# Products of probabilities and values in the opposite order within a batch

## The chip, the cores and the metric

The kernel runs on one core of one Trainium2 chip. The metric is the device time of one execution in microseconds. The kernel before takes 1553.61 us, the median of three runs (1551.71 to 1553.72).

## What is computed

Two layers of a streaming encoder. Each normalises its input, projects it, sends the projection through three parallel groups (a short convolution, latent attention with 8 heads, an RWKV-7 recurrence), gates each group, projects the concatenated output and adds the input. There are 1104 rows: 64 of a running stream with 256 cached rows, 16 meta rows and 1024 rows of a new stream. The change touches the last step of the attention:

```
s = jnp.where(vis[None, None], s, NEG)
p = jax.nn.softmax(s, axis=-1).astype(v.dtype)
return jnp.einsum('bhqk,bkhd->bqhd', p, v)
```

Attention is causal over chunks of 64 rows, so a query block sees all key blocks up to its own. Head width of the values is 64. Everything is float32.

## The kernel before

The heads are taken in four pairs. For a pair, the queries come in five units: u = -1 (the 64 rows of the running stream and the 16 meta rows) and u = 0 to 3 (256 rows each). Four generators of `attention` work on these: `scores` makes the scores of one head and unit, their maximum, exponential and scaling, and leaves probability tiles `p` with queries on the partitions; `transpose` turns them with TensorE into a PSUM bank `tr`, one bank for each job, and evicts the bank to a tile `pt` with keys on the partitions; `outputs` multiplies `pt` with the values `v` into the PSUM tile `po`; `prepare` makes keys, queries and values.

`jobs(u)` lists what is multiplied: for u >= 0 the meta keys, then 2u + 1 blocks of 128 keys that both halves of the 256 queries see (256 columns of `po`), then one block that only the later 128 queries see (columns 128 to 256). For u = -1 there are three entries in two jobs, all over 80 columns. So a pair has 20 entries of 256 columns, 4 of 128 and 3 of 80; with four pairs and two layers that is 160, 32 and 24. Each entry needs two products, one for each head of the pair: head j = 0 goes to partitions 0 to 63 of `po`, j = 1 to 64 to 127. That makes 432 products; a float32 product stands as two records in the trace.

`outputs` takes the jobs of a unit in batches of at most BATCH = 5, here called goes: 3 jobs in one go for u = 0, 5 for u = 1, 4 and 3 for u = 2, 5 and 4 for u = 3, 2 for u = -1. A pair has 7 goes, the program 56. JOBS = 7 tiles `pt` exist. Once the unit is done, VectorE multiplies `po` with the gate into `yo`, which is written to memory; the output projection reads it back later (`yraw`).

Two things set the order. First the generators are stepped by the program's own estimate of when things are due (`race`, `due`, class Meter), so that a go is recorded as one piece; `fill` is the part of the output projection that needs no attention (`prj<-yhi,wo` and `prj<-ylo,wo`), taken where nothing else is due. Then the framework under it schedules the recorded instructions on each engine's queue: of those that it takes to be ready it issues the one that was recorded first, so that a recorded piece can be taken apart. All instructions go through one helper, so line 81 stands for nearly all of them, and tiles' names tell them apart.

Of the kernel before, what the change touches and what calls it, by code (L numbers as in the profile page):

```python
# [194 lines left out]
class Net:  # L195
# [518 lines left out]
    def attention(self, l):  # L714
# [113 lines left out]
        def jobs(u):  # L828

            if u < 0:  # L830
                n = PAD0
                return [[(0, 128, 0, n, 0, True, False), (1, 128, 2 * n, n, 0, False, False)], [(2, n, 0, n, 0, False, True)]]
            x = [[(3, 128, 0, 256, 0, True, False)]]
            x += [[(4 + k, 128, 0, 256, 0, False, False)] for k in range(2 * u + 1)]
            return x + [[(4 + 2 * u + 1, 128, 0, 128, 128, False, True)]]
# [23 lines left out]

        def outputs():  # L860
            for pr, u in units:
                todo, po = jobs(u), None
                while todo:
                    size = -(-len(todo) // -(-len(todo) // BATCH))
                    batch, todo = todo[:size], todo[size:]
                    blocks = [b for js in batch for b, *_ in js]
                    yield (lambda: len(turned) >= count["jobs"] + size and all((pr, 4 * (b // 4) if b > 3 else 0 if b < 2 else b) in valued for b in blocks),)
                    ts = turned[count["jobs"]:count["jobs"] + size]
                    yield *ts, *(self.v[b][:k] for js in batch for b, k, *_ in js), *(() if po else ("po",))
                    po = po or self.ps("po", "po")  # L870
                    for t, js in zip(ts, batch):
                        for b, k, c, m, o, start, stop in js:
                            for j in range(2):
                                r = slice(64 * j, 64 * j + 64)
                                self.mm(po[r, o:o + m], self.v[b][:k, r], t[:, c + j * m:c + (j + 1) * m], start=start, stop=stop)
                    count["jobs"] += size
                q0, n = span(u)
                yo = self.small("yo", [128, 256], bufs=2)
                nc.vector.tensor_tensor(out=yo[:, :n], in0=po[:, :n], in1=gates[pr, u][:, :n], op=ALU.mult)
                nc.sync.dma_start(self.yd[4 + pr, :, q0:q0 + n], yo[:, :n])  # L880
                count["out"] += 1
# [653 lines left out]
```

## Time and profile before

| | |
|---|---|
| median of three runs | 1553.61 us |
| the profiled execution | 1553.56 us |
| its span, first to last instruction | 1551.8 us |
| matmuls on TensorE | 1476.9 us, 95% of the span |
| VectorE, ScalarE, GpSimd | 69%, 50%, 17% |
| mean granted TensorE clock | 0.989 |

Attention's products stand in two stretches of the span, one in each layer: about 466 to 710 us and 1228 to 1470 us. A record of a matmul has a start that was measured and an end that is modelled, so times below are taken from a record's start to the start of the next one.

### The profile page before, as it was taken

To read this page: it belongs to the slowest core of one execution; us is meant where nothing else is said; L and a number is where in the kernel's file an instruction comes from. 1 tells how busy PE (TensorE), PEld (TensorE's weight loads), DVE (VectorE), ACT (ScalarE), POOL (GpSimd) and SP (SyncE) were. 2 spreads that over 40 slices of the span, in tenths; PEclk is the share of its full clock that TensorE was granted. 3 is DMA by queue.
4 is the path that set the end of the run, shared out by engine and by line. 5 is a ranking of instruction groups with operands and counts; after the bars stand their busy time and mean duration, and the time that the engine had idled before them with its cause. 6 is when DMAs were issued, how large, how long until landed. Compare 5 with 4: busy or idle time off the path is not lost.

```text
span 1551.8 us, 30755 instructions
## 1 busy us (share of the span) xinstructions
PE 1476.9 (95%) x12060; PEld 1311.2 (84%) x12060; DVE 1065.6 (69%) x2623; ACT 769.8 (50%) x1842; POOL 256.5 (17%) x281
## 2 busy tenths in 40 slices
PE   7999998998999999999999998899999999999996
PEld 7988887987887878879999887798988878778795
DVE  7576596675868766675845575776867787676566
ACT  7135454444577565563522354444356775565442
POOL 0221221311221101100011222312212301011002
PEclk9999999999999999999999999999999999999998
DMA  6332112222324101211323311212222331102123
GB/s 218 123 113 68 52 54 60 83 52 57 92 94 152 38 26 33 68 57 62 147 93 103 110 45 49 70 48 81 69 65 65 115 120 46 31 19 84 47 65 117
DMA packets 95328, 119.82 MB, mean 77 GB/s; under 512 B 41872, under 2 KB 74768, under 8 KB 95184
## 3 DMA queue, kind: packets, MB, share of 16 engines
q1 hardware_dynamic: 95184, 117.87, 24.6%
q8 instruction: 95, 1.56, 0.4%
q14 instruction: 49, 0.40, 0.1%
HBM read 81.24 MB, written 36.60 MB: 76 GB/s over the span
## 4 chain that ended last, share of the span: by engine, by line
PE 65%; DVE 17%; ACT 7%; issue 5%; DMA 3%; POOL 2%; SPq 0%; DVEq 0%; POOLq 0%; ACTq 0%
PE prj L81 31%; PE sc L81 7%; PE po L81 7%; PE tr L81 5%; PE upq L81 3%; DVE tri L81 3%; PE inv L81 2%; DVE wq L81 2%; PE val L81 1%; DVE wlo L81 1%; ACT wq L81 1%; PE upk L81 1%; DVE st L81 1%; DVE cv L81 1%; PE w L81 1%
## 5 line engine op out<-in xcount | busy, mean ns | idle before, releaser
L81 PE MATMUL prj<-hhi,whi 128*128 128x384 f32 (+1 forms) x1152 | 391.7, 340 | 7.5 <-ACT hhi L81 6.6
L81 PE MATMUL prj<-hlo,whi 128*128 128x384 f32 (+1 forms) x1152 | 390.7, 339 | 0.6 <-DVE hlo L81 0.6
L81 PE MATMUL prj<-hhi,wlo 128*128 128x384 f32 (+1 forms) x1152 | 390.4, 339 | 0.2 <-DVE wlo L81 0.2
L81 PEld LDWEIGHTS prj<-hhi,whi 128*128 128x128 f32 x1152 | 218.9, 190 | 11.0 <-ACT hhi L81 6.6
L81 PEld LDWEIGHTS prj<-hlo,whi 128*128 128x128 f32 x1152 | 218.7, 190 | 4.9 <-DVE hlo L81 1.0
L81 PEld LDWEIGHTS prj<-hhi,wlo 128*128 128x128 f32 x1152 | 218.7, 190 | 3.3 <-issue 0.5
L81 PE MATMUL prj<-yhi,wo 128*128 128x384 f32 (+2 forms) x776 | 207.0, 337 | 0.9 <-DVE xn L81 0.9
L81 PE MATMUL sc<-ka,qa 128*128 128x264 f32 (+8 forms) x720 | 152.4, 334 | 2.3 <-ACT p L81 2.0
L81 ACT ACTIVATE p<-sc,st 128x144 f32<-128x144 f32 (+8 forms) x240 | 128.1, 542 | 50.4 <-DVE st L81 49.3
L81 PEld LDWEIGHTS prj<-yhi,wo 128*128 128x128 f32 x776 | 138.4, 188 | 4.8 <-DVE xn L81 2.4
L81 DVE TENSOR_REDUCE st<-sc 128x1 f32<-128x144 f32 (+8 forms) x240 | 118.0, 502 | 24.3 <-PE sc L81 22.4
L81 PE MATMUL prj<-ylo,wo 128*128 128x384 f32 (+2 forms) x388 | 130.6, 337 | 0.0
L81 ACT ACTIVATE pt<-tr 128x512 f32<-128x512 f32 (+3 forms) x172 | 90.0, 544 | 77.6 <-PE tr L81 76.3
L81 PEld LDWEIGHTS sc<-ka,qa 128*128 128x128 f32 (+1 forms) x720 | 112.2, 187 | 19.0 <-ACT p L81 6.1
L81 PE MATMUL tr<-cst,p 128*128 128x128 f32 (+2 forms) x752 | 115.7, 277 | 3.3 <-ACT pt L81 1.7
L81 PE MATMUL po<-pt,v 128*64 128x256 f32 (+3 forms) x864 | 110.7, 357 | 0.0
L81 PEld LDWEIGHTS tr<-cst,p 128*128 128x128 f32 (+2 forms) x752 | 83.5, 140 | 25.6 <-issue 7.6
L81 POOL TENSOR_TENSOR qa<-qt,qa 128x512 fp32r<-128x512 f32 (+1 forms) x40 | 47.3, 1184 | 349.3 <-ACT qa L81 349.3
L81 ACT ACTIVATE whi<-wraw 128x1024 fp32r<-128x1024 f32 x48 | 50.7, 1056 | 82.6 <-PE prj L81 64.9
L81 DVE TENSOR_TENSOR tri<-tri 48x14 f32<-48x14 f32 (+6 forms) x336 | 82.2, 245 | 9.1 <-DMA tri<-tri 0.3
L81 PEld LDWEIGHTS po<-pt,v 128*64 128x64 f32 (+1 forms) x864 | 56.6, 136 | 33.5 <-issue 11.6
L81 DVE TENSOR_SCALAR p<-p,st 80x336 f32<-80x336 f32 (+5 forms) x144 | 81.5, 568 | 1.9
(227 smaller groups left out, 2639.9 us busy)
## 6 DMA issues: line engine op xcount, KB each, us to landing
wraw<-w_in SPq DMA_DIRECT2D x48, 512.0 KB, 3.6
wraw<-w_out SPq DMA_DIRECT2D x32, 256.0 KB, 2.6
zd<-z SPq DMA_DIRECT2D x14, 576.0 KB, 3.4
wr<-zd SPq DMA_DIRECT2D x36, 192.0 KB, 3.0
gd<-gate SPq DMA_DIRECT2D x12, 552.0 KB, 3.1
yraw<-yd SPq DMA_DIRECT2D x8, 552.0 KB, 4.0
xn<-x SPq DMA_DIRECT2D x8, 552.0 KB, 3.9
xd<-xn SPq DMA_DIRECT2D x8, 552.0 KB, 3.0
```

The lines of the kernel that those rows point to most:

```text
L81: r = f(*args, **kw)
```

## The change

Within a go the entries are taken in the opposite order: the newest tile first, the oldest last. The start flag, which clears the accumulator, is now set on the first product of a unit for each of the two heads (`seen`), and the stop flag on the last product of the unit; the check of accumulation groups at build time is off for these products, since the first product of some units covers only columns 128 to 256.

```
-                todo, po = jobs(u), None
+                todo, po, seen = jobs(u), None, set()
...
-                    for t, js in zip(ts, batch):
-                        for b, k, c, m, o, start, stop in js:
-                            for j in range(2):
-                                r = slice(64 * j, 64 * j + 64)
-                                self.mm(po[r, o:o + m], self.v[b][:k, r], t[:, c + j * m:c + (j + 1) * m], start=start, stop=stop)
+
+                    xs = [(t, *x) for t, js in zip(ts, batch) for x in js][::-1]
+                    for i, (t, b, k, c, m, o, _, _) in enumerate(xs):
+                        for j in range(2):
+                            r = slice(64 * j, 64 * j + 64)
+                            self.mm(po[r, o:o + m], self.v[b][:k, r], t[:, c + j * m:c + (j + 1) * m], start=j not in seen,
+                                    stop=not todo and i == len(xs) - 1, group=False)
+                            seen.add(j)
```

The order of TensorE's instructions around it changes as well. The first place is the second go of unit u = 2 of the first pair in the first layer: `po_5658` is its accumulator, `pt_5630`, `pt_5656` and `pt_5670` its tiles in the order of their making, `tr_5667` the bank that is evicted to `pt_5670`. Before:

```order
L81 MATMUL tr_5667<-cst,p_5418 128x128
L81 MATMUL tr_5667<-cst,p_5493 128x128
L81 MATMUL prj_5647<-yhi_5621,wo_5246 128x336
L81 MATMUL po_5658<-pt_5630,v_5033 64x256
L81 MATMUL sc_5679<-ka_4791,qa_5296 128x16
L81 MATMUL sc_5679<-ka_4792,qa_5296 128x16
L81 MATMUL sc_5679<-ka_4791,qa_5296 128x16
L81 MATMUL po_5658<-pt_5630,v_5033 64x256
L81 MATMUL po_5658<-pt_5656,v_5033 64x256 x2
L81 MATMUL po_5658<-pt_5670,v_5033 64x128 x2
```

At the same place the changed kernel has:

```order
L81 MATMUL tr_5667<-cst,p_5418 128x128
L81 MATMUL tr_5667<-cst,p_5493 128x128
L81 MATMUL sc_5679<-ka_4791,qa_5296 128x16
L81 MATMUL sc_5679<-ka_4792,qa_5296 128x16
L81 MATMUL sc_5679<-ka_4791,qa_5296 128x16
L81 MATMUL upq_5722<-cqhi_4996,uq_5444 128x336
L81 MATMUL upq_5722<-cqlo_4998,uq_5444 128x336
L81 MATMUL upq_5722<-cqhi_4996,uq_5444 128x336
L81 MATMUL po_5658<-pt_5670,v_5033 64x128 x2
L81 MATMUL po_5658<-pt_5656,v_5033 64x256 x2
L81 MATMUL po_5658<-pt_5630,v_5033 64x256 x2
```

The go stood in two pieces, with one product of `pt_5630` on each side of a score, and stands in one now; query products (`upq`) moved in front of it.

The second place is on TensorE too, near the end of the first layer's attention: the second go of unit u = 3 of the last pair, with `po_8008`, and `pt_8029` as its newest tile, evicted from `tr_8026`. Before:

```order
L81 MATMUL tr_8026<-cst,p_7874 128x128
L81 MATMUL tr_8026<-cst,p_7924 128x128
L81 MATMUL prj_7963<-yhi_5621,wo_7275 128x384
L81 MATMUL po_8008<-pt_7998,v_5033 64x256 x2
L81 MATMUL po_8008<-pt_8006,v_5033 64x256 x2
L81 MATMUL po_8008<-pt_8024,v_5033 64x256 x2
L81 MATMUL po_8008<-pt_8029,v_5033 64x128 x2
```

The changed kernel has there:

```order
L81 MATMUL tr_8026<-cst,p_7874 128x128
L81 MATMUL tr_8026<-cst,p_7924 128x128
L81 MATMUL prj_7963<-yhi_5621,wo_7275 128x384
L81 MATMUL prj_7963<-ylo_5622,wo_7275 128x384
L81 MATMUL prj_7963<-yhi_5621,wo_7275 128x384
L81 MATMUL po_8008<-pt_8029,v_5033 64x128 x2
L81 MATMUL po_8008<-pt_8024,v_5033 64x256 x2
L81 MATMUL po_8008<-pt_8006,v_5033 64x256 x2
L81 MATMUL po_8008<-pt_7998,v_5033 64x256 x2
```

The go was one piece and still is, in the opposite order; between the last transposition of its newest tile and the product of that tile stood a projection and six products, and now three projections.

Over the whole program, the products stand in 100 runs (stretches of TensorE's order with no other matmul between them) before and in 60 now; 44 and 8 of these hold an odd number of products.

## Rows read from the trace of the kernel before

**Rows 1.** The page's head and busy shares of each engine.

```profile
span 1551.8 us, 30755 instructions
...
PE 1476.9 (95%) x12060; PEld 1311.2 (84%) x12060; DVE 1065.6 (69%) x2623; ACT 769.8 (50%) x1842; POOL 256.5 (17%) x281
```

**Rows 2.** The page's chain that ended last, by engine.

```profile
PE 65%; DVE 17%; ACT 7%; issue 5%; DMA 3%; POOL 2%; SPq 0%; DVEq 0%; POOLq 0%; ACTq 0%
```

**Rows 3.** Busy time by stretch: length, then each engine, PEclk, DMA share, GB/s.

```profile
466.00:710.00 244.00, 240.80 (x1705) 190.67 (x1705) 171.85 (x470) 143.11 (x397) 22.68 (x19) 1.00 0.20 61
...
1228.00:1470.00 242.00, 238.84 (x1694) 188.64 (x1694) 171.52 (x469) 143.51 (x396) 22.71 (x19) 1.00 0.20 62
```

**Rows 4.** Groups of the products and their weight loads: busy, mean ns | idle before.

```profile
L81 PE MATMUL po<-pt,v 128*64 128x256 f32 (+3 forms) x864 | 110.7, 357 | 0.0
...
L81 PEld LDWEIGHTS po<-pt,v 128*64 128x64 f32 (+1 forms) x864 | 56.6, 136 | 33.5 <-issue 11.6 <-ACT v L81 1.3 <-DVE wo L81 0.3
```

**Rows 5.** TensorE's timeline from 552.61: start us, us, what [idle before].

```profile
552.75 0.65 PE L81 MATMUL po<-pt,v 128*64 128x256 f32 x2
553.33 0.66 PE L81 MATMUL tr<-cst,p 128*128 128x128 f32 x4
```

**Rows 6.** The same from 700.29.

```profile
700.29 0.65 PE L81 MATMUL po<-pt,v 128*64 128x256 f32 x4
700.88 0.66 PE L81 MATMUL tr<-cst,p 128*128 128x128 f32 x4
701.47 1.94 PE L81 MATMUL po<-pt,v 128*64 128x256 f32 x14
703.34 0.88 PE L81 MATMUL tr<-cst,p 128*128 128x128 f32 x6
```

**Rows 7.** The same from 542.31 to 549.92.

```profile
542.31 0.66 PE L81 MATMUL tr<-cst,p 128*128 128x128 f32 x4
542.72 0.40 PE L81 MATMUL prj<-ylo,wo 128*128 128x336 f32 x1
542.96 0.47 PE L81 MATMUL prj<-yhi,wo 128*128 128x336 f32 x2
543.26 0.32 PE L81 MATMUL prj<-ylo,wo 128*128 128x336 f32 x1
543.42 0.47 PE L81 MATMUL prj<-yhi,wo 128*128 128x336 f32 x2
...
545.65 0.20 PE L81 MATMUL sc<-hide 128*128 128x64 bf16 x1
545.69 0.40 PE L81 MATMUL prj<-yhi,wo 128*128 128x336 f32 x1
...
547.69 0.20 PE L81 MATMUL sc<-hide 128*128 128x64 bf16 x1
547.83 2.17 PE L81 MATMUL po<-pt,v 128*64 128x256 f32 x20
549.92 0.50 PE L81 MATMUL sc<-ka,qa 128*128 128x16 f32 x3
```

**Rows 8.** Groups by shape: last transposition, evictions of probability tiles, exponential and its sum.

```profile
L81 PE MATMUL tr<-cst,p 128*128 128x128 f32 (+2 forms) x752 | 115.7, 277 | 3.3 <-ACT pt L81 1.7 <-DVE p L81 0.7 <-DVE st L81 0.3
...
L81 ACT ACTIVATE pt<-tr 128x512 f32<-128x512 f32 x128 | 73.9, 600 | 60.8 <-PE tr L81 60.4
...
L81 DVE COPY pt<-tr 128x512 f32<-128x512 f32 x32 | 22.1, 690 | 28.9 <-PE tr L81 28.6
...
L81 ACT ACTIVATE pt<-tr 128x256 f32<-128x256 f32 x28 | 11.0, 392 | 16.4 <-PE tr L81 15.7
...
L81 ACT ACTIVATE p<-sc,st 128x144 f32<-128x144 f32 (+8 forms) x240 | 128.1, 542 | 50.4 <-DVE st L81 49.3 <-ACT pt L81 0.2
...
L81 ACT ACTIVATION_READ_ACCUMULATOR p<-sc,st 128x1 f32 (+1 forms) x240 | 48.4, 202 | 0.0
```

**Rows 9.** Timeline of all engines around the first go.

```profile
465.98 0.61 ACT L81 ACTIVATE pt<-tr 128x320 f32<-128x320 f32 x2
...
466.77 0.64 PE L81 MATMUL po<-pt,v 128*64 128x80 f32 x12
```

**Rows 10.** Waits of TensorE's weight loads, 466 to 710: us, times, longest.

```profile
PEld tr L81 <- ACT pt L81: 3.9, 10, 1.0
...
PEld sc L81 <- ACT p L81: 3.0, 7, 0.6
```

**Rows 11.** DMA issues on SP: count, KB each, median us to landing.

```profile
yraw<-yd SPq DMA_DIRECT2D x8, 552.0 KB, 4.0
```

## The prediction

> **What bounds the kernel now.** I read the busy shares first: TensorE's matmuls fill 95% of the span, VectorE 69%, ScalarE 50% [rows 1]. The chain of waits says the same: TensorE holds 65% of it, VectorE 17%, ScalarE 7% [rows 2]. Then the table by stretch, for the two stretches in which products of probabilities and values run, 466 to 710 us and 1228 to 1470 us: 240.8 of 244 us and 238.8 of 242 us are matmul time, at the full granted clock, 1.00, while VectorE has 172 and ScalarE 143 [rows 3]. So in the stretches that the change touches, TensorE's own list of work sets the end, and what shortens that list is worth nearly its whole length, as long as nothing that it waits for is late.
>
> The groups give the products 864 records (two records for each of the 432 products; every key block needs two products, one for the upper and one for the lower 64 rows of the output) and 110.7 us busy, with 0.0 us of idle matmul time ahead of them [rows 4]. Their weight loads were idle 33.5 us before, and 11.6 us of that ended with nothing to wait for ("issue"); evictions of probability tiles do not stand among the releasers there [rows 4]. So no product waited for a tile before, and a wait is not what the change can remove.
>
> The timeline shows what it can remove. A run is a stretch of product records with nothing else between them. One lone product (2 records) takes 0.58 us from its start to the next instruction, 552.75 to 553.33 [rows 5]; two products (4 records) take 0.59 us, 700.29 to 700.88 [rows 6]. The upper and the lower product of a block run beside each other, so one that stands alone costs as much as a pair. Seven products (4 begun pairs) take 1.87 us, 701.47 to 703.34 [rows 6]: three more pairs for 1.28, or 0.43 each. That leaves 0.16 us at a run's end that no pair explains (0.59 less 0.43). The run of ten, 547.83 to 549.92, fits: 0.16 + 4 x 0.43 + half for its 128-column pair makes 2.10, and the rows say 2.09 [rows 7].
>
> A run also costs something at its start. Four transpositions with a projection behind take 0.41 us (542.31 to 542.72) [rows 7], and with products behind them 0.59 (700.88 to 701.47) [rows 6]: 0.18 more. From a score's mask (hide) to a projection it is 0.04 us, 545.65 to 545.69, and to a product 0.14, 547.69 to 547.83 [rows 7]: 0.10 more.
>
> **The change, part by part.** The arithmetic stays: the same 432 products, transpositions and evictions. The start and stop flags move with the order and add no instruction. What changes is the order that comes out. With the oldest tile first, a go's first product is free long before its last tile is there, and the scheduler puts it where it is free, one by one among scores and transpositions. With the newest tile first, nothing of a go is free until the newest tile is, and the go stands together. Counted in the two orders of TensorE: 100 runs before, 60 now; runs of an odd number of products 44 before, 8 now; single products 26 before, none now.
>
> Half-filled pairs: an odd run wastes half a pair. There are (44 - 8) / 2 = 18 pairs fewer, at 0.43: 7.7 us.
>
> Ends of runs: 40 fewer at 0.16: 6.4 us.
>
> Starts of runs: of those that go, 25 stood behind transpositions and 14 behind scores, and one net behind something else: 25 x 0.18 + 15 x 0.10 = 6.0 us. This term is the least sure, because other neighbours now meet (transposition and score more often); its ends are 0 and 40 x 0.18 = 7.2.
>
> That is 20.1 us less of TensorE's list. As a check, all 100 runs by this formula (160 pairs of 256 columns at 0.43, 32 of half, 24 of 80 columns at 0.14, 22 lost pairs, 100 ends) come to 104.7 us, beside the 110.7 of the group, whose ends are modelled [rows 4].
>
> The Trainium skill ("TensorEngine Tiling (Array Packing)", Tiling Modes, Key Properties) says that a change of tiling mode drains the engine, whatever the neighbours are. By that rule a start behind a score should cost as much as one behind a transposition, and the sum would be 40 x 0.18 + 14.1 = 21.3 us. The rows show 0.10 against 0.18, so I keep them apart.
>
> What is given back comes in two parts. First, the added wait: the go's first product now waits for the newest tile, and behind it in TensorE's queue stand the next transpositions and scores, so VectorE's maxima and ScalarE's exponentials wait with it. The newest tile is mostly the one of 128 columns, whose eviction takes 0.39 us on ScalarE; wide ones take 0.60 there or 0.69 on VectorE [rows 8]. From an eviction's end to its product it was 0.18 us (465.98 + 0.61 to 466.77) [rows 9]. With 0.28 for the last transposition [rows 8] the way is some 0.9 us where ScalarE is free. Before, at least 8 records stood between a tile's last transposition and its first product; now it is 3 at the tightest (twice), at most 7 in 14 of the 60 runs and at most 13 in 24. Three projections are 0.46 us (542.96 to 543.42) [rows 7]: some 0.3 short. With ScalarE always free the loss is near 1 us in all. With an exponential (0.54 us and 0.20 for its sum) [rows 8] ahead of the eviction in all 24 it is 24 x 0.74 = 17.8. ScalarE is busy 59% of the stretch, and the order puts most last evictions directly behind the ones before: I take half of an exponential in 13 of 24, 3.5 us.
>
> Second, the softmax round trip (scores, maximum, exponential, scaling, transposition) has 10 us less of TensorE's work beside it per layer. Of the waits in the first stretch, transpositions' loads waited 3.9 us for tile evictions, scores' loads 3.0 us for exponentials [rows 10]; with the smaller ones it is some 15 us in 244. I take 1.5 us more per layer, 3.0; ends 0 and 10 (half of the gain).
>
> No transfer ends late, I think: SP's queue only has a weight load ahead of a residual load at a few places. After the last product of a layer 24 and 26 projections are left of the stage's filling, 33 and 34 before, at 0.15 each (0.46 for three) some 4 us; the output projection behind them takes the last unit's columns only in its third group, 72 projections or 11 us later, and the read back from memory takes 4.0 us [rows 11].
>
> Sum: -20.1 + 3.5 + 3.0 = -13.6 us. The profiled execution took 1553.56 us (span 1551.8 [rows 1] and 1.8 around it); the median of the three runs is 1553.61, the same within 0.1. So 1540.0.
>
> **Rivals.** (a) The barrier rules, and the kernel gets slower. TensorE takes its matmuls in order, so a go that waits holds everything. If in the 24 tight places the eviction itself is queued behind a whole exponential, each costs 0.54 + 0.20 + 0.39 = 1.13 us, 27.1 in all, and the time is 1553.6 - 20.1 + 27.1 = 1560.6. It decides above 20.1 / 24 = 0.84 us a place. For it: nothing of the go can cover the wait any more. Against it: matmul idle before products was 0.0, and projections held for filling now stand in such places. The Trainium skill ("PSUM — Partial Sum Buffer", Engine vs sequencer instructions) supports the first step: matmuls start and complete in program order. Chance 5%.
>
> (b) The softmax chain rules in these stretches: what TensorE saves it then waits. Half lost to it: 1553.6 - 10 + 3.5 = 1547.1, chance 20%. All lost: 1553.6, chance 7%. For it: the loads' waits above. Against it: VectorE at 172 of 244 us.
>
> (c) Nothing is given back: 1553.6 - 20.1 = 1533.5, chance 13%.
>
> That the goes aren't joined can be left out: the order shows them.
>
> **How the numbers follow.** Forecast 55%, 1536 to 1545 by itself. With (a) 5%, (b) 27%, (c) 13%: faster 0.55 + 0.20 + 0.13 = 0.88; no change, within 0.2% (3.1 us, about what a measurement of this kernel can tell), 0.07; slower 0.05. The range goes from (c) to a little beyond the half of (b): 1533 to 1550.
>
> **What would show it.** In the profile after, the products' group should have some 14 us less busy time than 110.7, with lone products gone from the timeline; the weight loads' "issue" idle before products, 11.6, should fall to about 60% of it. The stretches of rows 3 should each be some 7 us shorter, with the rest of the program unmoved. Idle time before products with an eviction as its releaser should be near 3.5 us. If it is over 10, (a) is at work; if scores and transpositions wait some 10 us more, (b) is. If the products' busy time stays at 110, the price of a run is wrong, and with it the forecast.

## The result, and the profile after

The changed kernel takes 1536.07 us, the median of four runs (1533.82 to 1538.76), beside 1553.66 (1551.71 to 1555.56) for the kernel before on the same chip. The ratio is 0.9885, with a 95% interval of 0.9870 to 0.9900: 17.6 us less. The prediction was 1540.0, with a range of 1533 to 1550. The profiled execution took 1536.26 us, 17.3 less than that of before (1553.56).

The page's head, busy shares and chain after, which answer to [rows 1, 2]:

```profile
span 1534.3 us, 30679 instructions
...
PE 1459.0 (95%) x12060; PEld 1306.4 (85%) x12060; DVE 1063.0 (69%) x2623; ACT 769.3 (50%) x1842; POOL 258.0 (17%) x281
...
PE 65%; DVE 17%; ACT 8%; issue 5%; DMA 3%; POOL 2%; SPq 0%; DVEq 0%; ACTq 0%; POOLq 0%
```

The span is 17.5 us shorter and TensorE's matmul time 17.9 us; the count of its instructions is the same, 12060, and every share is as it was within a point. So the kernel is still bound by TensorE's list of work, and the list got shorter. The table by stretch shows where. First the kernel before, the stretches that [rows 3] left out (length, then each engine's busy time and count, the granted clock, DMA):

```profile
0.00:466.00 466.00, 434.74 (x3948) 402.01 (x3949) 323.53 (x778) 223.85 (x493) 100.42 (x120) 0.99 0.29 89
...
710.00:1228.00 518.00, 494.82 (x4318) 463.65 (x4317) 347.66 (x818) 232.13 (x504) 99.65 (x111) 0.99 0.26 80
...
1470.00:1551.80 81.80, 67.73 (x403) 66.23 (x402) 51.01 (x92) 27.17 (x54) 11.06 (x12) 0.94 0.26 86
```

Then the changed kernel, all five stretches:

```profile
0.00:466.00 466.00, 434.97 (x3953) 401.99 (x3953) 324.26 (x781) 224.51 (x494) 100.48 (x120) 0.99 0.29 89
466.00:703.00 237.00, 233.21 (x1708) 189.52 (x1707) 170.83 (x467) 142.42 (x394) 23.35 (x19) 1.00 0.21 63
703.00:1220.00 517.00, 493.74 (x4315) 462.65 (x4314) 347.83 (x819) 232.66 (x507) 99.61 (x111) 0.99 0.26 81
1220.00:1454.00 234.00, 230.48 (x1698) 187.21 (x1697) 169.17 (x466) 142.38 (x395) 23.53 (x19) 1.00 0.20 63
1454.00:1534.30 80.30, 66.61 (x395) 64.99 (x394) 50.94 (x92) 27.33 (x54) 11.05 (x12) 0.93 0.27 89
```

The two stretches with products are 7.0 and 8.0 us shorter (244 to 237, 242 to 234), with the same number of instructions within 4, and what they lost is matmul time: 7.6 and 8.4 us. TensorE's idle time in them, the length less the matmul time, came to 6.4 us before (3.2 + 3.2, [rows 3]) and is 7.3 now (3.8 + 3.5), so 0.9 us more. The rest of the program, behind each of them, is 1.0 and 1.5 us shorter. The groups of the products, which answer to [rows 4]:

```profile
L81 PE MATMUL po<-pt,v 128*64 128x256 f32 (+3 forms) x864 | 94.3, 354 | 0.0
...
L81 PEld LDWEIGHTS po<-pt,v 128*64 128x64 f32 (+1 forms) x864 | 53.2, 136 | 26.3 <-issue 4.9 <-ACT pt L81 2.0 <-DVE v L81 1.3
```

The same 864 records are busy 94.3 us, 16.4 less than before. Their weight loads wait 4.9 us with no releaser (11.6 before), and a new releaser has come: the eviction of a tile on ScalarE, 2.0 us in all. TensorE's timeline around the go of ten products that [rows 7] show:

```profile
544.35 0.20 PE L81 MATMUL sc<-hide 128*128 128x64 bf16 x1
544.48 2.17 PE L81 MATMUL po<-pt,v 128*64 128x128 f32 x20
546.58 0.50 PE L81 MATMUL sc<-ka,qa 128*128 128x16 f32 x3
```

This go was whole before too: it took 2.09 us there and takes 2.10 here, and the mask (hide) ahead of it 0.14 and 0.13. A run costs what it did; there are fewer of them.

To see where the 17.5 us are, I summed the time from each record's start to the next one's start on TensorE, in both profiled executions, from the first product of a layer to its last. Of an instruction that stands just ahead of a product, its usual time ahead of something else (the median of its kind) is left with its kind, and only what goes beyond that is put down as the start of a run. A go's first product that waits for its tile makes this time longer, so the 3.5 us that the prediction counted for that wait stand in the row of starts:

| us, both layers | before | after | difference | predicted |
|---|---|---|---|---|
| products, to the next record (pairs and run ends) | 104.0 | 89.5 | -14.5 | -14.1 |
| starts of runs, with the wait for the newest tile | 13.9 | 8.4 | -5.5 | -2.5 (-6.0 + 3.5) |
| TensorE's other work but the filling | 288.3 | 289.8 | +1.5 | +3.0 |
| filling projections (365, then 382) | 71.8 | 76.4 | +4.6 | 0, with the row below |
| all that lies outside of this | 1073.8 | 1070.2 | -3.6 | |
| span | 1551.8 | 1534.3 | -17.5 | -13.6 |

How far such rows can be trusted shows in the first experiment below, whose kernel has the order of before: its four rows inside come to 104.0, 13.9, 288.5 and 71.8 us, within 0.2 of those of before, but what lies outside to 1077.4, 3.6 us more.

### The profile page after: what moved, and what is told of

Its sections match the earlier page's. It is cut to its first block, busy times and chain, and to the rows that moved or that the text cites. A ratio compares the mean times of both kernels' runs of the same rounds, so it can differ in the third digit from the quotient of the medians.

```text
span 1534.3 us, 30679 instructions
## 1 busy us (share of the span) xinstructions
PE 1459.0 (95%) x12060; PEld 1306.4 (85%) x12060; DVE 1063.0 (69%) x2623; ACT 769.3 (50%) x1842; POOL 258.0 (17%) x281
## 4 chain that ended last, share of the span: by engine, by line
PE 65%; DVE 17%; ACT 8%; issue 5%; DMA 3%; POOL 2%; SPq 0%; DVEq 0%; ACTq 0%; POOLq 0%
PE prj L81 33%; PE sc L81 6%; PE po L81 6%; PE tr L81 5%; DVE tri L81 3%; PE upq L81 3%; PE inv L81 3%; DVE wq L81 2%; PE val L81 1%; ACT wq L81 1%; DVE wlo L81 1%; DVE st L81 1%; PE upk L81 1%; PE tm L81 1%; PE w L81 1%
## 5 line engine op out<-in xcount | busy, mean ns | idle before, releaser
L81 DVE TENSOR_REDUCE st<-sc 128x1 f32<-128x264 f32 (+8 forms) x240 | 117.7, 502 | 23.5 <-PE sc L81 21.8
L81 PE MATMUL po<-pt,v 128*64 128x256 f32 (+3 forms) x864 | 94.3, 354 | 0.0
L81 DVE TENSOR_TENSOR wlo<-wraw,whi 128x1024 fp32r<-128x1024 f32 x48 | 67.8, 1412 | 12.7 <-ACT whi L81 12.2
```

The costliest lines, as they stand in the source:

```text
L81: r = f(*args, **kw)
```

## Experiments

The theory: the gain is TensorE's list, and it comes from the joined runs (fewer ends, starts and half-filled pairs), by the prices in the prediction. The rivals: the flags or the direction itself cost or save something; a run's price is not what the timeline suggests (products may be cheap or dear for another reason); what was given back is a wait for the newest tile. Ratios are to the kernel before on the same chip; its median there was 1555.58 us for the first four versions, 1554.57 for the next four and 1554.08 for the last two. Versions of different groups are compared by their ratios.

**The flags alone.** The old order with the new flags:

```
-                    xs = [(t, *x) for t, js in zip(ts, batch) for x in js][::-1]
+                    xs = [(t, *x) for t, js in zip(ts, batch) for x in js]
```

> Edit: the changed kernel's flags (start once for each head of a unit, one stop, no group check) with the old order within a go. TensorE's order is then the one of the kernel before: 100 runs of products, 44 odd. Joining theory: nothing of the gain is left, 1553.6 us, ratio to before 1.000 within 0.002. Rival (the flags, or fewer accumulation groups, save time by themselves): a part of the 17.5 us, so under 1550 us.

Measured: 1555.08 us, ratio 0.9996 (0.9984 to 1.0009). The products' group of this kernel:

```profile
L81 PE MATMUL po<-pt,v 128*64 128x256 f32 (+3 forms) x864 | 110.7, 358 | 0.0
```

110.7 us, as before the change. The flags cost no time. The clearing by a product of 128 columns only isn't tested here, since with the old order a unit's first product covers all its columns.

**Only the newest tile first.** The rest of the go in the old direction:

```
-                    xs = [(t, *x) for t, js in zip(ts, batch) for x in js][::-1]
+                    xs = [(t, *x) for t, js in zip(ts, batch) for x in js]
+                    xs = xs[-1:] + xs[:-1]
```

> Edit: only the newest tile is taken first, the others of the go follow in the old order, oldest to newest. TensorE's order has 60 runs, 8 odd, as in the changed kernel. Joining theory: the whole gain, 1536 us within 3 us. Rival (the opposite order as such matters, for instance because tiles come free in it or because the column halves follow each other otherwise): clearly slower than 1540 us.

Measured: 1537.29 us, ratio 0.9880 (0.9866 to 0.9895). TensorE's order has 60 runs, 8 odd, as in the changed kernel, and the group agrees to the last digit:

```profile
L81 PE MATMUL po<-pt,v 128*64 128x256 f32 (+3 forms) x864 | 94.3, 354 | 0.0
```

So the opposite direction does nothing by itself. What works is that the first product of a go needs the last tile.

**The second newest first, the newest last.** A step between the two kernels:

```
+                    xs = xs[-2:-1] + xs[:-2] + xs[-1:]
```

> Edit: the second newest tile is taken first and the newest last. TensorE's order has 77 runs, 38 odd. Joining theory, relative to the changed kernel: 17 more runs at 0.16 + 0.16 (end and start), 5.4 us, and 15 more half-filled pairs at 0.43, 6.5 us, so 1536 + 11.9 = 1548 us, the products' group some 12 us busier than the 94.3 us of the changed kernel. Rival (the wait for the newest tile is what matters, whether as cost or as gain): the time is at either end, 1536 or 1553 us, whatever the runs.

Measured: 1552.97 us, ratio 0.9983 (0.9971 to 0.9995), some 2.6 us less than before where 5.6 were expected (1553.6 less 1548). That is a miss, and the time is the one that the rival gave. The order holds 77 runs, 38 odd. The group and the weight loads' waits on evictions and scaled probabilities, 466 to 1480 us (engine, what for: us, times, longest):

```profile
L81 PE MATMUL po<-pt,v 128*64 128x256 f32 (+3 forms) x864 | 104.4, 355 | 0.2 <-ACT pt L81 0.2
```

```profile
PEld tr L81 <- ACT pt L81: 9.4, 28, 1.0
...
PEld tr L81 <- DVE p L81: 4.1, 11, 0.5
```

In the kernel before, these two waits in the same stretch were:

```profile
PEld tr L81 <- ACT pt L81: 7.3, 19, 1.0
...
PEld tr L81 <- DVE p L81: 2.3, 6, 0.5
```

The time alone doesn't tell the theory from the rival. But the group is 10.1 us busier than in the changed kernel, where the theory has 12 and the rival nothing. By the sums from start to start the products and starts fell by 8.6 us from those of before (4.7 and 3.9), in the size that the runs give; TensorE's other work rose by 3.4 and the filling inside the stretches by 4.3 (15 projections more). So the raw gain came and most of it went again, a larger share than in the changed kernel. Weight loads of transpositions wait longer for evictions and scaled probabilities, but the matmuls' own idle time ahead of transpositions is 4.2 us beside 3.3 before [rows 8], so these waits explain some 0.9 us of it:

```profile
L81 PE MATMUL tr<-cst,p 128*128 128x128 f32 (+2 forms) x752 | 117.0, 278 | 4.2 <-ACT pt L81 1.7 <-DVE p L81 1.3 <-DVE st L81 0.3
```

Its profiled execution was the slowest of its ten (1557.56, mean granted clock 0.986 beside 0.989 in before), so the sum doesn't close on its median, and I don't put a number on the waits.

**A pair taken apart.** To test that a product must stand beside its neighbour of the other head, one product of the second pair was moved to the go's end, in the changed kernel:

```
+                    ys = [(j, x) for x in xs for j in range(2)]
+                    ys = ys[:3] + ys[4:] + ys[3:4]
```

> Edit: in each go the second entry's product for head 1 is moved to the go's end, so that no run is added (60 runs) but one pair of each go no longer stands side by side. Joining theory: 48 goes lose a pair of 256 columns (0.43 us each), 8 one of 80 columns (0.14): 20.6 + 1.1 = 21.8 us, less 0.9 for two odd runs fewer, so 1536 + 21 = 1557 us. Rival (products beside each other do not matter, only the number of runs does): 1536 us.

Measured: 1542.29 us, ratio 0.9915 (0.9897 to 0.9932). That is a miss: far from 1557, and only some 4.7 us above the changed kernel (0.9915 less 0.9885, of 1555.6), about as little as the two intervals can tell apart. Its four runs lie between 1537.08 and 1544.36 us, and the profiled one is the fastest of them. The products' group, and the go of ten that stood at 544.48 above:

```profile
L81 PE MATMUL po<-pt,v 128*64 128x256 f32 (+3 forms) x864 | 97.8, 357 | 0.0
```

```profile
543.08 0.20 PE L81 MATMUL sc<-hide 128*128 128x64 bf16 x1
543.22 2.22 PE L81 MATMUL po<-pt,v 128*64 128x128 f32 x20
545.36 0.50 PE L81 MATMUL sc<-ka,qa 128*128 128x16 f32 x3
```

2.14 us instead of 2.10. Behind the place where the order is shifted, the starts of records follow each other by 56 and 160 ns in turn, where they follow by 7 and 209 ns in the changed kernel: another pattern, with the same 216 ns for two records. So products of the two heads share time although they are not the two of one block, at least with one head a place ahead of the other, which is all that was tried. The picture that fits this run, and the odd switch below, is that a run costs by the number of products of the head that has more of them, not by the number of blocks whose two products stand together. For the change both pictures give the same numbers (an odd run has one product more for one head), so the term holds, but my reason for it was too narrow.

**A switch in every go.** The price of an end and a start by itself: in the changed kernel, one small matmul over the whole array (a mask of 64 columns, into columns of `po` that nothing reads) behind the fourth product of every go, so that whole pairs stand on either side:

```
+                        if i == 1:
+                            self.mm(po[:, 448:512], self.hide[:, 0:128], self.hide[:, 128:192], start=False, stop=False, group=False)
```

> Edit: in the changed kernel one small matmul over the whole array (the mask's 128 x 64, bf16, into unread columns of the accumulator) stands in every go behind the fourth product; it splits the run between two full pairs. TensorE's order has 120 runs, 16 odd, against 60 and 8. Joining theory, relative to the changed kernel: 60 ends at 0.16 (9.6 us), 60 starts, 56 of them behind a mask at 0.10 (6.3), 56 small matmuls at 0.04 (2.2), 4 half-filled pairs (1.7): 19.8 us more, a ratio to before near 1.001 where the changed kernel has 0.9885. Rival (ends and starts of runs cost nothing, only lone products do): 3.9 us more, 0.991.

Measured: 1556.00 us, ratio 1.0004 (0.9989 to 1.0018). The whole gain is gone, with goes that are still recorded newest first.

**The same switch, one product earlier,** behind the third, so that nearly every run is odd:

```
+                            if i == 1 and j == 0:
+                                self.mm(po[:, 448:512], self.hide[:, 0:128], self.hide[:, 128:192], start=False, stop=False, group=False)
```

> Edit: as the last one, but the small matmul stands behind the third product, so that it splits a pair: 118 runs, 112 odd. The moved product of the broken-pair experiment still ran beside a neighbour of the other head; here the other head has nothing in the run to go beside. Joining theory with the price of a half-filled pair: 48 more of them at 0.43 (some at less), 20 us over the last one, a ratio near 1.013. Rival (a lone product costs only its own share, as the broken pairs suggested): the same time as the last one within 4 us.

Measured: 1573.49 us, ratio 1.0115 (1.0092 to 1.0137), 17.5 us above the even switch. The products' groups of the even and of the odd switch:

```profile
L81 PE MATMUL po<-pt,v 128*64 128x256 f32 (+3 forms) x864 | 108.8, 361 | 0.0
```

```profile
L81 PE MATMUL po<-pt,v 128*64 128x256 f32 (+3 forms) x864 | 126.5, 361 | 0.0
```

The even switch has 120 runs, 16 odd, the odd one 118, 112 odd. From start to start, 60 runs more than in the changed kernel cost 10.5 us at the products (89.5 to 100.0) and 7.6 us at the starts (8.4 to 16.0), the masks' own time among the latter. By the prediction's prices the products should have cost 60 x 0.16 + 4 x 0.43 = 11.3. The 48 further half-filled pairs cost 17.8 us (100.0 to 117.8), 0.37 each where 0.43 is the price of a pair of 256 columns; some of these are narrower. Both prices are shown: 0.37 for a half-filled pair, and with that 0.15 for an end (10.5 less 4 x 0.37, over 60), which the prediction had at 0.16.

**A go one tile later.** Is what was given back a wait for the newest tile? In the changed kernel, a go is recorded only once one more tile is turned:

```
-                    yield (lambda: len(turned) >= count["jobs"] + size and ...
+                    yield (lambda: len(turned) >= min(count["jobs"] + size + 1, 104) and ...
```

> Edit: in the changed kernel a go is recorded only when one more tile than it needs has been turned, so that its newest tile is evicted well before its first product. TensorE's order then has 86 runs, 40 odd; places with at most 13 records between last transposition and first product: 12 instead of 24. Joining theory: 26 more runs at 0.32 (8.3 us) and 16 more half-filled pairs (6.9), less some 2 us of waits: 13 us more than the changed kernel, a ratio near 0.997. Rival (the wait for the newest tile is the main thing given back, and the runs do not matter): faster than the changed kernel, a ratio under 0.987.

Measured: 1544.58 us, ratio 0.9932 (0.9912 to 0.9951). Runs were not kept: 86, 40 odd, so it is slower than the changed kernel, as expected, but by 7.3 us (0.9932 less 0.9885) and not by 13. The group, and the loads' waits on exponentials and evictions, 466 to 1480 us:

```profile
L81 PE MATMUL po<-pt,v 128*64 128x256 f32 (+3 forms) x864 | 105.3, 356 | 0.0
```

```profile
PEld tr L81 <- ACT pt L81: 4.8, 19, 0.4
...
PEld sc L81 <- ACT p L81: 4.3, 14, 0.6
```

And in the changed kernel, the same view:

```profile
PEld sc L81 <- ACT p L81: 8.2, 19, 0.8
...
PEld tr L81 <- ACT pt L81: 4.5, 16, 0.5
...
PEld po L81 <- ACT pt L81: 2.0, 6, 0.4
```

Products and starts cost 98.7 + 14.5 us, 15.3 more than after the change, and half of that is won again elsewhere. The wait of products for tiles is gone, and the one of scores for exponentials is half. So a later go does relieve waits of weight loads, as the rival said, but the runs that it breaks cost more.

**Goes of up to seven jobs,** BATCH = 7 in place of 5: 54 runs, 8 odd.

> Edit: in the changed kernel a go may hold seven tiles instead of five, so that unit u = 2 has one go instead of two (u = 3 still has two, of 5 and 4). 54 runs instead of 60, 8 odd as before. Joining theory: 6 runs less at 0.32, 2 us faster than the changed kernel, a ratio near 0.987. Rival (all seven tiles are taken by one go, and no next transposition can be evicted before it): slower than the changed kernel by 2 us or more.

Measured: 1536.88 us, ratio 0.9883 (0.9864 to 0.9902). Products and starts fell by a further 2.1 us (97.9 to 95.8), as 6 runs fewer should give; in the time it isn't to be told from the changed kernel.

**Eight tiles and goes of seven,** with `gt` and `yo` in one buffer each to make room:

```
-JOBS = 7
-BATCH = 5
+JOBS = 8
+BATCH = 7
```

> JOBS = 8 tiles instead of 7, goes of up to seven jobs instead of five, and to make room the tiles gt and yo in one buffer instead of two; the rest as in the changed kernel. TensorE's order holds 54 runs instead of 60, 8 odd ones as before it. Theory (a run's end and start are what is paid, about 0.16 + 0.15 us; the first product's wait for the newest tile is paid once a go): 6 runs fewer give 1.9 us, two goes of unit 3 become... one or two fewer waits for a newest tile per pair, 0.3: some 1534 us, ratio to the kernel before 0.987. Rival (the eighth tile lets transpositions go ahead and takes away most of the 3.4 us that transpositions and scores lost in the changed kernel): 1531 us or below, ratio 0.985. Other rival (the single buffers of gt and yo put VectorE's last multiplication of a unit behind the write of the one before): 1540 us or above.

Measured: 1535.32 us, ratio 0.9874 (0.9849 to 0.9899). Its sums from start to start are those of the run before within 0.3 us in every row. The intervals of the two and of the changed kernel overlap: no gain that these runs can show. The rival with 1540 us (0.991) lies outside the interval, the one with 1531 (0.985) at its lower edge, so that one isn't excluded.

**Products stepped before transpositions,** the first two names in ORDER exchanged:

> Only the order in which the four generators are stepped changes: products before transpositions, where both are due. The changed kernel otherwise. TensorE's order has the same 60 runs, 8 odd. Theory (what was given back is the round trip of the softmax and the wait for the newest tile; a go recorded earlier than the next transposition is issued earlier only if its newest tile is there): within 2 us of the changed kernel, 1536 us, ratio 0.9887. Rival (the go stands in the way of transpositions, whose evictions then come late, and stepping it first makes that worse): 1540 us or above, ratio 0.991.

Measured: 1536.04 us, ratio 0.9880 (0.9858 to 0.9903). The 60 runs and their 89.5 + 8.4 us are unmoved. One view of the loads' waits, 466 to 1480 us, is not:

```profile
PEld po L81 <- ACT pt L81: 4.9, 17, 0.4
...
PEld po L81 <- DVE pt L81: 1.1, 4, 0.4
```

The products' weight loads now wait for an eviction 21 times, 6.0 us in all, instead of 6 times and 2.0 us. The matmuls themselves were idle for 0.2 us ahead of products:

```profile
L81 PE MATMUL po<-pt,v 128*64 128x256 f32 (+3 forms) x864 | 94.3, 354 | 0.2
```

So nearly all of these waits lay beside matmuls that were still running. That the time is the same doesn't show it by itself, for other work moved as well: 522 filling projections stand inside the stretches instead of 382 (102.0 us instead of 76.4), and 21 us less lies outside.

No version beat the changed kernel by more than these runs can tell.

## Why the prediction was right, and where its size was off

**What bounds the kernel.** Right. The time followed TensorE's list in both stretches, at a granted clock of 1.00 in both kernels, while VectorE's and ScalarE's work stayed as it was.

**Half-filled pairs and ends, 7.7 + 6.4 = 14.1.** Measured 14.5. The even and the odd switch show each price alone. The taken-apart pair corrects the reason: a half-filled pair is time in which one head has no product left in the run, also where the two products of a block don't stand together.

**Starts, 6.0.** Measured 5.5, and its two prices hold about: in the trace of before 55 runs stand behind transpositions at 0.169 us each, in the one of after 30 at 0.167, where the prediction has 0.18; behind a mask it is 0.094 in both (12 and 6 of them), for 0.10. The neighbours that now meet instead, which made this term the least sure one, brought no price that shows. The Trainium skill ("TensorEngine Tiling (Array Packing)", Tiling Modes, Key Properties) says that changing the tiling mode drains TensorE. From that the prediction worked out 21.3 us for the raw gain, with one price for every start, beside its own 20.1. With 14.5 + 5.5 = 20.0 measured, and starts that cost 0.094 or 0.167 by what stands ahead, the trace doesn't bear out one price for all.

**Given back, 3.5 + 3.0.** This is the term that was mis-sized, and it makes nearly all of the 3.9 us between 1540.0 and 1536.1. The first part, the wait for the newest tile, hardly shows. A releaser stands there that did not before, with 2.0 us on the weight loads, six times. But the matmuls have 0.0 us idle ahead of products, and the starts of runs after the change, at the prices that the same neighbours had before, would come to 8.0 us by my estimate and came to 8.4. That leaves at most some 0.4 us for the wait. I had counted half an exponential, 0.27 us, in 13 of 24 places; the loads waited in six, and there the matmuls ahead were still running. With two generators exchanged the loads waited 6.0 us, and the matmuls were idle for 0.2. The second part, the softmax round trip, had 3.0 us, and TensorE's other work came to +1.5; in the two stretches TensorE idles 0.9 us more in all. Scores' loads wait longer for exponentials (6.1 us before, 8.2 after, from the same view), transpositions' loads shorter for evictions (7.3, now 4.5). I had set the filling at nothing. 17 projections moved into the stretches, which got 4.6 us longer by them, and outside there are 3.6 us less; the 1.0 between them is less than what lies outside moves by from one execution to another, so no cost is shown.

**The rivals.** (a), a barrier that costs more than it saves, needed 0.84 us a place and found some 0.4 us in all. (b), the softmax chain, is excluded by the interval (its 1547.1 would be 0.9958). (c), nothing given back, had 1533.5 us, a ratio of 0.987, which is the interval's lower end; the forecast's 1540.0 would be 0.991, outside of it. So the time alone doesn't exclude (c), and that something was given back rests on the sums. The 55% were for 1536 to 1545 us, and 1536.07 lies just inside, so this one term used up nearly all of the margin. The tests named in the prediction came out as they should for the gain, with the busy time 16.4 lower for 14, "issue" 42% of what it was for 60%, and the stretches 7.0 and 8.0 shorter for 7. Idle time before products with an eviction as its releaser was 2.0 us on the loads for 3.5, and none on the matmuls.

**Open.** Why the second newest tile first gives back most of its gain, while the newest first gives back an eighth at most, isn't settled: the idle time ahead of transpositions explains 0.9 us, and the sum doesn't close. Nor is it which of the waits relieved by the later go were worth its 7 us. And the taken-apart pair costs 3.5 us more at the products, 0.06 in each go, and some 4.7 us in the time; I have no reason for these.

## What to carry to other kernels

Where a full engine takes its work in order, count the stretches of one kind in its order before and after a change, and price their ends, starts and half-filled places from the timeline: here that gave the raw gain to 0.1 us (20.1 for 20.0), in part by luck, since its two rows were off by 0.4 and 0.5 in opposite directions. A piece of work that must not be taken apart is kept together by naming the input that comes last first. Count a new wait on a weight load as a loss only where the matmuls are idle behind it.

## What the runs showed of the hardware

Two products that each use one half of the array's columns run beside each other also when they are not the two of one block: with one head a place ahead of the other, two records still took 216 ns (56 + 160 in place of 7 + 209), and a run of ten 2.14 us in place of 2.10.

A small matmul over the whole array in the midst of such a run is dear for its size: 56 of them, whose own time behind other work is 0.04 us [rows 7], took the ratio from 0.9885 to 1.0004, some 0.33 us each, and to 1.0115, some 0.64 each, where they also part a pair.
